# Feed-forward: where the two Silus of a part's first pair stand on ScalarE

## The chip, the cores and the metric

The kernel runs on one core of one Trainium2 chip. The metric is the device time of one execution in microseconds, the median of several runs. The names of the engines are those of the profile: PE is TensorE (PEld its weight loads), DVE is VectorE, ACT is ScalarE, POOL is GpSimd, SP is SyncE, which issues the loads.

## The reference

Two sequences (256 and 512 tokens, width 1024) go through two layers. Each layer has a mixer (an mLSTM in layer 0, a sliding-window attention in layer 1) and then a gated feed-forward with a depthwise convolution over three tokens:

```python
def conv_ffn(h, w_up, conv_w, conv_b, w_down):
    u = h @ w_up                                  # 1024 -> 2 * 2816
    u = lax.conv_general_dilated(u, conv_w[:, None, :], ...) + conv_b
    g = u[..., :D_FF]
    val = u[..., D_FF:]
    return (jax.nn.silu(g) * val) @ w_down
```

Around it stand a modulated RMS norm and a residual: `x = x + g2 * conv_ffn(h, ...)`. All is fp32. The kernel reaches that precision on PE by splitting each operand in two parts (`whi`/`wlo` for weights, `zh`/`zl` and others for activations) and taking three products of four.

## The kernel before, in words

The 768 tokens are one row of columns. The 2816 channels of the gate and the 2816 of the value are cut into 11 **parts** of 256 channels. A part `p` does, in `up(p)`, two **pairs**: pair 0 is the gate's 256 channels, pair 1 the value's. Then, one part later, `down(*prev)` multiplies the finished product of the part before with its 256 rows of `w_down` and adds it to the residual.

A pair (`pair`, line 1272) computes two output rows of 128 channels for all 768 columns by a Strassen-like scheme with seven products. A product is a call of `quarters`: 12 matmuls of 128x384 (lines 1252, 1253, 1254: high by high, low by high, high by low). The names T1, T2, T3, T4, B11, B21, B22 stand for the seven right-hand quarters; `yh/yl` hold B11 and B21, `zh/zl` hold T1 to T4, `bq` holds B22. The products gather in four fixed PSUM banks, `a`, `e`, `b`, `d` (in the order lists below `ps_4595`, `ps_4596`, `ps_4597`, `ps_4598`). Three copies on ACT fork a running sum into another bank or out of it. In the order of the code of a pair with its own B11 (all parts but the first two):

- `a` takes B11; the first fork `b <- a` (line 1296) starts `b`.
- `e` takes T1, and `p5 <- e` (line 1301) keeps it.
- `b` takes T2; then **`d <- b` (line 1307)**, which T3 must wait for, since `d` gathers T3 on top of it.
- `a` takes B21 and is evicted by ACT (line 1260, two pieces).
- `d` takes T3, and **`u3 <- d` (line 1315)**, the pair's third copy; meanwhile `b` takes B22.
- DVE writes the second halves of the two rows (lines 1317 and 1318); `d` takes T4 and ACT evicts it (line 1260).

A scheduler that plans with a timeline orders each engine's instructions from the code's order and the data dependences, so the code's order is a wish, not the final row. It interleaves pairs with the `down` tiles of the part before (line 230, PSUM tiles `pa`, four buffers, evicted into the residual by DVE at line 690). `tc.issue_after(ins)` makes what is written inside it stand behind `ins`. Weights come through five `raw` buffers of 128x1024; `split` makes `whi` by a cast on ACT (line 236) and `wlo` by a subtraction on DVE (line 237). POOL makes the sums of weight quarters (lines 1280 to 1292).

Behind each pair, `up` runs the convolution for its two rows: one activation on ACT (line 1476) and two scalar_tensor_tensor on DVE (lines 1478, 1479) for a row. For pair 0 the two rows of the gate, `yrow[:, 0]` and `yrow[:, 1]`, then get a Silu in place on ACT (line 1503). For pair 1 POOL multiplies each row of the value with the Silu of the gate (line 1505), and the product is split into `g` (lines 236 and 237), which `down` reads one part later.

Part 0 is written out by hand (`head`) and takes no `pair`. Part 1's pairs have `rest=True`: their B11 and B21 were done early.

Of the kernel before, what the change touches and what calls it, by code (L numbers as in the profile page):

```python
# [12 lines left out]
AF = mybir.ActivationFunctionType  # L13
# [65 lines left out]
def col(t):  # L79

    return t + (GAP if t >= 256 else 0)
# [64 lines left out]
class Net:  # L146
# [1125 lines left out]
    def pair(self, pool, u, bank, rows, rest=False):  # L1272


        nc = self.nc
        r1, r2 = rows
        rb, ra = (self.load(u, h) for h in (1, 0))
        q = [t[:, 512 * i : 512 * (i + 1)] for t in (ra, rb) for i in range(2)]
        tt = nc.gpsimd.tensor_tensor
        tt(q[2], q[2], q[3], ALU.add)  # L1280
        if not rest:
            wa = self.split(ra)
        tt(q[0], q[2], q[0], ALU.subtract)  # L1283
        tt(q[1], q[1], q[0], ALU.subtract)
        s1h, s1l = (pool.tile([P, 512], R, tag=t, name=self.nm(t), bufs=1) for t in ("s1h", "s1l"))
        part = lambda w, i: [t[:, 512 * i : 512 * (i + 1)] for t in w]
        fork = r1[:, col(H) :]
        if not rest:
            fork = a = bank(0)
            self.quarters(a, part(wa, 0), self.B11, True)  # L1290
        self.fp_copy_split(s1h, s1l, q[2])
        tt(q[2], q[3], q[0], ALU.subtract)
        wc = self.split(ra)
        wb = self.split(rb)
        e, b = bank(1), bank(2)
        nc.scalar.copy(b, fork)
        p5 = self.tmp([P, H])

        def fifth():
            self.quarters(e, (s1h, s1l), self.T1, True)  # L1300
            nc.scalar.copy(p5, e)

        if not rest:
            fifth()
        self.quarters(b, part(wc, 0), self.T2, False)
        d = bank(3)
        nc.scalar.copy(d, b)  # L1307
        if rest:
            fifth()
        else:  # L1310
            self.quarters(a, part(wa, 1), self.B21, False)
            self.evict(r1, a)
        self.quarters(d, part(wb, 0), self.T3, False)
        u3 = self.tmp([P, H])
        nc.scalar.copy(u3, d)
        self.quarters(b, part(wc, 1), self.B22, False)
        nc.vector.tensor_tensor(r1[:, col(H) :], b, p5, ALU.add)
        nc.vector.tensor_tensor(r2[:, col(H) :], e, u3, ALU.add)
        self.quarters(d, part(wb, 1), self.T4, False)
        self.evict(r2, d)  # L1320

    def prepare(self, u0, l):

        flat = [z.rearrange("p j k t -> p (j k t)") for z in (self.zh, self.zl)]
        place = lambda j: [z[:, j : j + 1024] for z in flat]

        ahead = [place(12 * H), place(4 * H)]
        wa = place(0)
        spare = None
        if l:  # L1330

            spare = self.slab([P, 3072], R)
            wa = [spare[:, 1024 * (z + 1) : 1024 * (z + 2)] for z in range(2)]
        self.fp_copy_split(*wa, self.load(u0 + 1, 0))
        for i in range(0 if l else 2):
            self.fp_copy_split(*ahead[i], self.load(u0 + 3 + i, 0))
        return wa, ahead, spare
# [123 lines left out]
    def ffn(self, l, xt, pool, last_tile, apply, keep=None):  # L1461
        nc = self.nc
        u0 = U_FFN + l * NPART * 3
        early = self.prepare(u0, l)
        next(last_tile)

        urows = [self.slab([P, 4, TG]) for _ in range(2)]
        for urow in urows:
            nc.gpsimd.memset(urow[:, :, 256 : 256 + GAP], 0.0)

        behind = []

        def conv(u, y, ch):
            cb = self.cst(CB + l * 44 + ch)
            w = lambda tap: self.cst(CW + (l * 44 + ch) * 3 + tap)
            nc.scalar.activation(y, u, AF.Identity, bias=cb, scale=w(1))  # L1476
            stt = nc.vector.scalar_tensor_tensor
            stt(y[:, 1:], u[:, :-1], w(0), y[:, 1:], ALU.mult, ALU.add)  # L1478
            stt(y[:, :-1], u[:, 1:], w(2), y[:, :-1], ALU.mult, ALU.add)  # L1479

        def up(p):
            urow = urows[0] if p == 0 else urows[1]
            fixed = lambda i: self.bank[i][:, :H]
            if p == 0:
                eng = mybir.EngineType
                self.ready(HALVES[0])
                with self.tc.manual_schedule(engines={eng.PE, eng.Activation, eng.DVE}):
                    behind[:] = self.head(u0, last_tile, pool, urows, mark, early)
            for i in range(2):
                if p:  # L1490
                    rows = [urow[:, 2 * i + j] for j in range(2)]
                    with ExitStack() as order:
                        for ins in behind[2 * i :] if p == 1 else ():
                            order.enter_context(self.tc.issue_after(ins))
                        self.pair(pool, u0 + 3 * p + i, fixed, rows, rest=p == 1)
                if i == 0:
                    yrow = self.slab([P, 4, TG])
                    g = self.slab([P, 2, 2, TG], R)
                for j in range(2):
                    y = yrow[:, 2 * i + j]  # L1500
                    conv(urow[:, 2 * i + j], y, i * FC + 2 * p + j)
                    if i == 0:
                        nc.scalar.activation(y, y, AF.Silu)
                    else:
                        nc.gpsimd.tensor_tensor(y, y, yrow[:, j], ALU.mult)  # L1505
                        self.fp_copy_split(g[:, 0, j], g[:, 1, j], y)
            return g

        def mark(t):

            hi, _ = self.quarter(self.B11)
            self.mm(t, hi[0][:, :P], hi[0], True, True)

        def down(p, g):
            ws = (w for _, w in self.halves(u0 + 3 * p + 2))
            chunk = lambda w, i: [t[:, 512 * i : 512 * (i + 1)] for t in w]

            def tile(w, c, rng):
                s0, s1, _ = rng
                o = self.pa()[:, : s1 - s0]  # L1520
                cs = slice(c % 4 * P, (c % 4 + 1) * P)
                for i in range(2):
                    wh, wl = chunk(w, i)
                    gh, gl = (g[:, z, i, col(s0) : col(s0) + s1 - s0] for z in range(2))
                    self.mm(o, wh[:, cs], gh, i == 0, False)
                    self.mm(o, wh[:, cs], gl, False, False)
                    self.mm(o, wl[:, cs], gh, False, i == 1)
                self.resid(xt, o, l, 40, c, rng)

            if p < NPART - 1:  # L1530
                for h, w in enumerate(ws):
                    for rng in SAMPLE, PROMPT:
                        for c in range(4 * h, 4 * h + 4):
                            tile(w, c, rng)
                return
            ws = list(ws)
            for rng in RANGES:
                norm = Norm(self, xt, rng, apply, last=keep is None and rng is RANGES[-1], adds=None if keep is not None else nc.vector)
                for c in range(KC):
                    tile(ws[c // 4], c, rng)  # L1540
                    norm.square(c)
                    if keep is not None or rng is not RANGES[-1] or c < 3:
                        self.tick(0.65)
                if keep is not None:
                    self.save_x(xt, keep, rng)
                self.start(rng, norm.stages())

        prev = None
        for p in range(NPART):
            g = up(p)  # L1550
            if prev is not None:
                down(*prev)
            prev = (p, g)
        down(*prev)
# [175 lines left out]
```

## Time and profile before

| | |
|---|---|
| Runs | 1902.64, 1899.25, 1902.51 us; median 1902.51 us |
| Profiled execution | span 1900.1 us; no time beside the span is listed for it, and the median of the runs lies 2.4 us above this span |
| PE busy | 1812.0 us (95%) |
| DVE, ACT, POOL busy | 1413.8, 920.9, 491.0 us |
| Granted PE clock, mean | 0.983 |
| Silus (line 1503) | 44, mean 847 ns, 37.3 us in all |

The page gives the busy time of each engine, then the span in 40 slices, the DMA queues, the chain of waits that ended last, and groups of instructions by line. A group's row names the line, the engine, what is written and read, the number of instructions, the busy time, the mean of one in ns, the idle time of that engine just before them, and what ended most of that idle time. In a timeline each row is: start, duration, engine, line, operation, names, count, and in brackets the idle time before it with its releaser. Ends of matmuls are modelled, so an idle time of PE is counted from a modelled end.

### The profile page before, as it was taken

How to read it: one execution, taken by the hardware profiler on the slowest of the kernel's cores; microseconds unless marked ns; L12 is line 12 of the kernel's file. 1: busy time of each engine (PE TensorE's matmuls, PEld its weight loads, DVE VectorE, ACT ScalarE, POOL GpSimd, SP SyncE). 2: the span in 40 equal slices, each digit the busy share in tenths (PEclk: the TensorE clock that was granted, in tenths of full speed). 3: DMA queues.
4: the chain of work that ended last, by engine and by line, in shares of the span. 5: the costliest groups of instructions: out<-in, count | busy, mean ns of one | idle time of the engine just before them, and what ended most of it. 6: DMA issues, size and time to landing. Idle time of an engine off the chain costs nothing.

```text
span 1900.1 us, 29288 instructions
## 1 busy us (share of the span) xinstructions
PE 1812.0 (95%) x11354; PEld 1672.5 (88%) x11354; DVE 1413.8 (74%) x2310; ACT 920.9 (48%) x1849; POOL 491.0 (26%) x395
## 2 busy tenths in 40 slices
PE   7889999999999999999999999989989999999997
PEld 5787887888998999999999988879979999999996
DVE  4664776687589877777777768875998777777777
ACT  4633434343456444444444466773564444444443
POOL 3001000022013433333332303330133333333322
PEclk9888999999999999999999999999999999999998
DMA  8243655456412222222222321212222222222211
GB/s 321 66 141 113 210 166 165 153 167 199 144 55 89 67 67 67 67 67 67 67 67 79 112 81 48 84 58 90 78 78 77 68 67 67 67 67 67 67 34 67
DMA packets 64246, 184.49 MB, mean 97 GB/s; under 512 B 6167, under 2 KB 23831, under 8 KB 64108
## 3 DMA queue, kind: packets, MB, share of 16 engines
q1 hardware_dynamic: 64108, 182.63, 29.6%
q8 instruction: 89, 1.46, 0.3%
q14 instruction: 49, 0.40, 0.1%
HBM read 176.17 MB, written 6.43 MB: 96 GB/s over the span
## 4 chain that ended last, share of the span: by engine, by line
PE 76%; DVE 11%; issue 5%; ACT 4%; DMA 2%; POOL 2%; SPq 0%; POOLq 0%; ACTq 0%; DVEq 0%
PE pa L230 23%; PE ps L230 23%; PE ps L1252 10%; PE ps L1253 9%; PE ps L1254 9%; DVE wlo L237 2%; DMA bt<-brow 1%; DVE slab L690 1%; ACT t L1078 1%; DVE t L1069 1%; POOL nt L112 1%; DVE slab L1479 1%; DVE zl L1210 1%; DVE slab L1478 0%; DVE slab L237 0%
## 5 line engine op out<-in xcount | busy, mean ns | idle before, releaser
L236 ACT CAST whi<-raw 128x1024 fp32r<-128x1024 f32 x237 | 248.7, 1049 | 401.1 <-PE pa L230 200.3
L237 DVE TENSOR_TENSOR wlo<-raw,whi 128x1024 fp32r<-128x1024 f32 x237 | 330.7, 1395 | 113.5 <-ACT whi L236 112.8
L230 PE MATMUL pa<-slab,whi 128*128 128x256 f32 (+1 forms) x1472 | 344.8, 331 | 4.4 <-DVE slab L690 4.2
L230 PEld LDWEIGHTS pa<-slab,whi 128*128 128x128 f32 x1472 | 250.9, 188 | 31.4 <-DVE slab L690 5.8
L690 DVE SCALAR_TENSOR_TENSOR slab<-pa,mod,slab 128x256 f32<-128x256 f32 (+1 forms) x368 | 207.8, 592 | 67.5 <-PE pa L230 66.9
L230 PE MATMUL ps<-zh,whi 128*128 128x256 f32 (+2 forms) x688 | 233.6, 340 | 4.4 <-ACT whi L236 2.6
L230 PE MATMUL pa<-slab,wlo 128*128 128x256 f32 (+1 forms) x736 | 234.0, 330 | 0.0
L230 PE MATMUL ps<-zh,wlo 128*128 128x256 f32 (+2 forms) x688 | 228.6, 335 | 4.3 <-DVE wlo L237 4.3
L230 PE MATMUL ps<-zl,whi 128*128 128x256 f32 (+2 forms) x688 | 229.0, 334 | 1.6 <-DVE zl L536 0.9
L1252 PE MATMUL ps<-zh,whi 128*128 128x384 f32 x504 | 171.2, 340 | 14.3 <-ACT ps L1307 13.1
L1253 PE MATMUL ps<-zl,whi 128*128 128x384 f32 x504 | 169.8, 337 | 1.7 <-DVE zl L1210 1.7
L1254 PE MATMUL ps<-zh,wlo 128*128 128x384 f32 x504 | 169.0, 335 | 0.0
L230 PEld LDWEIGHTS pa<-slab,wlo 128*128 128x128 f32 x736 | 138.3, 188 | 13.0 <-DVE wlo L237 0.9
L230 PEld LDWEIGHTS ps<-zh,whi 128*128 128x128 f32 x688 | 132.7, 193 | 18.0 <-ACT whi L236 3.2
L230 PEld LDWEIGHTS ps<-zh,wlo 128*128 128x128 f32 x688 | 132.4, 192 | 15.1 <-DVE wlo L237 5.1
L230 PEld LDWEIGHTS ps<-zl,whi 128*128 128x128 f32 x688 | 132.5, 193 | 11.2 <-DVE zl L536 1.3
L1505 POOL TENSOR_TENSOR slab<-slab 128x772 f32<-128x772 f32 x44 | 83.3, 1893 | 206.7 <-DVE slab L1479 193.9
L1283 POOL TENSOR_TENSOR raw<-raw,raw 128x512 f32<-128x512 f32 x40 | 52.1, 1303 | 294.1 <-DVE wlo L237 244.1
L1478 DVE SCALAR_TENSOR_TENSOR slab<-slab,cstt,slab 128x771 f32<-128x771 f32 x88 | 105.3, 1199 | 26.9 <-ACT slab L1476 26.9
L1479 DVE SCALAR_TENSOR_TENSOR slab<-slab,cstt,slab 128x771 f32<-128x771 f32 x88 | 119.7, 1360 | 0.8
L472 DVE SCALAR_TENSOR_TENSOR ada<-raw,silc,ada 128x1024 f32<-128x1024 f32 x84 | 114.0, 1387 | 6.5 <-DMA raw<-in_adaln_w_dram 6.3
L1252 PEld LDWEIGHTS ps<-zh,whi 128*128 128x128 f32 x504 | 94.7, 188 | 22.2 <-ACT ps L1307 18.2
(309 smaller groups left out, 4182.4 us busy)
## 6 DMA issues: line engine op xcount, KB each, us to landing
raw<-in_w_dram SPq DMA_DIRECT2D x208, 512.0 KB, 3.7
raw<-in_adaln_w_dram SPq DMA_DIRECT2D x84, 512.0 KB, 4.4
slab<-in_x_dram SPq DMA_DIRECT2D x12, 512.0 KB, 7.6
slab<-in_adaln_w_dram SPq DMA_DIRECT2D x12, 512.0 KB, 10.9
slab<-mrows SPq DMA_DIRECT2D x8, 384.0 KB, 5.7
xs<-slab SPq DMA_DIRECT2D x6, 512.0 KB, 2.9
bt<-brow SPq DMA_DIRECT2D x16, 192.0 KB, 3.2
slab<-xs SPq DMA_DIRECT2D x6, 512.0 KB, 6.7
```

What stands on the lines that cost most here:

```text
L230: self.last_mm = self.nc.tensor.matmul(out, lhsT, rhs, start=start, stop=stop)
L236: nc.scalar.copy(hi, src)
L237: return nc.vector.tensor_tensor(lo, src, hi.bitcast(F32), ALU.subtract)
L472: stt(acc[:, s], row, w, acc[:, s], ALU.mult, ALU.add)
L690: self.nc.vector.scalar_tensor_tensor(x, o, self.mod[l][:, gc + c, q : q + 1], x, ALU.mult, ALU.add)
L1252: mm(o, wh[:, k], hi[k], start=start and k == 0, stop=False, skip_group_check=True)
L1253: mm(o, wh[:, k], lo[k], start=False, stop=False, skip_group_check=True)
L1254: mm(o, wl[:, k], hi[k], start=False, stop=k == 3, skip_group_check=True)
L1283: tt(q[0], q[2], q[0], ALU.subtract)
L1478: stt(y[:, 1:], u[:, :-1], w(0), y[:, 1:], ALU.mult, ALU.add)
L1479: stt(y[:, :-1], u[:, 1:], w(2), y[:, :-1], ALU.mult, ALU.add)
L1505: nc.gpsimd.tensor_tensor(y, y, yrow[:, j], ALU.mult)
```

## The change

The two Silus of pair 0 are no longer written behind that pair's convolution, but behind the whole of pair 1's `pair` call, ahead of pair 1's convolution. In the parts from 1 on they stand inside `issue_after(third)`, where `third` is pair 1's third copy (`u3 <- d`), which `pair` now returns. In part 0, which has no `pair`, they are only written later.

```diff
         self.quarters(d, part(wb, 0), self.T3, False)
         u3 = self.tmp([P, H])
-        nc.scalar.copy(u3, d)
+        third = nc.scalar.copy(u3, d)
         self.quarters(b, part(wc, 1), self.B22, False)
...
         self.evict(r2, d)
+        return third.ins
...
-                        self.pair(pool, u0 + 3 * p + i, fixed, rows, rest=p == 1)
+                        third = self.pair(pool, u0 + 3 * p + i, fixed, rows, rest=p == 1)
                 if i == 0:
                     yrow = self.slab([P, 4, TG])
                     g = self.slab([P, 2, 2, TG], R)
+                if i:
+                    with self.tc.issue_after(third) if p else ExitStack():
+                        for j in range(2):
+                            nc.scalar.activation(yrow[:, j], yrow[:, j], AF.Silu)
                 for j in range(2):
                     y = yrow[:, 2 * i + j]
                     conv(urow[:, 2 * i + j], y, i * FC + 2 * p + j)
-                    if i == 0:
-                        nc.scalar.activation(y, y, AF.Silu)
-                    else:
+                    if i:
                         nc.gpsimd.tensor_tensor(y, y, yrow[:, j], ALU.mult)
                         self.fp_copy_split(g[:, 0, j], g[:, 1, j], y)
```

In the changed file the lines behind 1315 carry numbers higher by 1 to 3; the convolution is at 1477, 1479 and 1480, the Silu by chance at 1503 again.

The order of the instructions shows what the scheduler made of it. First ACT in part 7 of layer 0, pair 1 (`slab_8119` holds that part's `yrow`; `s1h_8412` is the cast of the next pair's weight sum; `whi_8263` and `whi_8333` are the two halves of `w_down` for the part before). Before:

```order
L1503 ACTIVATE slab_8119<-slab_8119 128x772
L236 CAST whi_8161<-raw_8129 128x1024
L1260 COPY slab_5199<-ps_4598 128x128
L1260 COPY slab_5199<-ps_4598 128x256
L1476 ACTIVATE slab_8119<-slab_5199,cstt 128x772
L236 CAST s1h_8412<-raw_8401 128x512
L1301 COPY nt_8166<-ps_4596 128x384
L1503 ACTIVATE slab_8119<-slab_8119 128x772
L1307 COPY ps_4598<-ps_4597 128x384
L236 CAST whi_8263<-raw_8261 128x1024
L1260 COPY slab_5199<-ps_4595 128x128
L1260 COPY slab_5199<-ps_4595 128x256
```

The third copy (line 1315) and the cast `whi_8333` are the next two rows there. In the changed kernel the same place reads:

```order
L236 CAST s1h_8412<-raw_8401 128x512
L1301 COPY nt_8164<-ps_4596 128x384
L1307 COPY ps_4598<-ps_4597 128x384
L236 CAST whi_8263<-raw_8261 128x1024
L1260 COPY slab_5199<-ps_4595 128x128
L1260 COPY slab_5199<-ps_4595 128x256
L1315 COPY nt_8217<-ps_4598 128x384
L1503 ACTIVATE slab_8119<-slab_8119 128x772 x2
L236 CAST whi_8333<-raw_8331 128x1024
L1477 ACTIVATE slab_8119<-slab_5199,cstt 128x772
```

The first Silu left its place between two weight casts, the second its place right ahead of `d <- b` (line 1307); both now stand between the third copy and the cast `whi_8333`. The same holds in parts 3 to 9 of both layers. From the middle of part 2's first pair on, the rows of PE, DVE, POOL and SP are, names aside, the same as before, up to the last `down` of the layer.

Second, DVE behind part 1's pairs, where `down` of part 0 runs between them and part 2's first pair (`wlo_6018` and `s1l_6131`, later `s1l_6129`, are weights of part 2; `pa` are the tiles of `down`). Before:

```order
L690 SCALAR_TENSOR_TENSOR slab_4605<-pa_5933,mod_88,slab_4605 128x512
L690 SCALAR_TENSOR_TENSOR slab_4605<-pa_5941,mod_88,slab_4605 128x512
L237 TENSOR_TENSOR wlo_6018<-raw_5991,whi_6017 128x1024
L690 SCALAR_TENSOR_TENSOR slab_4605<-pa_5949,mod_88,slab_4605 128x512
L690 SCALAR_TENSOR_TENSOR slab_4605<-pa_5957,mod_88,slab_4605 128x256
L237 TENSOR_TENSOR slab_5738<-slab_5737,slab_5738 128x772
L690 SCALAR_TENSOR_TENSOR slab_4605<-pa_5965,mod_88,slab_4605 128x256
L690 SCALAR_TENSOR_TENSOR slab_4605<-pa_5973,mod_88,slab_4605 128x256
L237 TENSOR_TENSOR s1l_6131<-raw_6119,s1h_6130 128x512
```

And in the changed kernel:

```order
L690 SCALAR_TENSOR_TENSOR slab_4605<-pa_5933,mod_88,slab_4605 128x512
L237 TENSOR_TENSOR wlo_6018<-raw_5991,whi_6017 128x1024
L237 TENSOR_TENSOR s1l_6129<-raw_6117,s1h_6128 128x512
L690 SCALAR_TENSOR_TENSOR slab_4605<-pa_5941,mod_88,slab_4605 128x512
L690 SCALAR_TENSOR_TENSOR slab_4605<-pa_5949,mod_88,slab_4605 128x512
L690 SCALAR_TENSOR_TENSOR slab_4605<-pa_5957,mod_88,slab_4605 128x256
L237 TENSOR_TENSOR slab_5738<-slab_5737,slab_5738 128x772
L690 SCALAR_TENSOR_TENSOR slab_4605<-pa_5965,mod_88,slab_4605 128x256
L690 SCALAR_TENSOR_TENSOR slab_4605<-pa_5973,mod_88,slab_4605 128x256
```

Two weight subtractions moved ahead of the eviction of `pa_5941`. The PE's row changes there too: T1 of part 2's first pair is done ahead of tile `pa_5941`, and part 1's T3 and B22 ahead of the second matmuls of a `down` tile. Layer 1 has the same. Beside these, PE, DVE and ACT rows are reordered from the last `down` of layer 0 into the attention's first projections, in the attention's softmax statistics (DVE) and slightly in the last norm.

## The prediction

> **What bounds the kernel now.** I read the page's busy shares first, then the waits of PE by stretch, then the timelines of ACT, PE and DVE at the places that the order list shows as changed.
>
> ```profile
> span 1900.1 us, 29288 instructions
> PE 1812.0 (95%) x11354; PEld 1672.5 (88%) x11354; DVE 1413.8 (74%) x2310; ACT 920.9 (48%) x1849; POOL 491.0 (26%) x395
> 640.00:1010.00 370.00, 364.74 (x2073) 345.59 (x2073) 283.50 (x317) 170.74 (x267) 132.67 (x78) 1.00 0.21 67
> 1480.00:1815.00 335.00, 329.75 (x1875) 312.50 (x1873) 258.08 (x287) 154.47 (x242) 120.38 (x72) 1.00 0.21 67
> ```
>
> The last two rows are windows over the steady feed-forward parts of layer 0 and layer 1: length, busy time of PE, PEld, DVE, ACT, POOL, then the granted clock. PE is missing 5.3 us in each, the clock is whole, and ACT works less than half of the time. So only what PE waits for counts there. The view of waits, PE alone, in the same two windows has one row each, and it accounts for all of the missing time:
>
> ```profile
> PE ps L1252 <- ACT ps L1307: 5.3, 7, 0.8
> PE ps L1252 <- ACT ps L1307: 5.3, 7, 1.0
> ```
>
> Seven times in each layer (parts 3 to 9, pair 1) T3's first matmul waits for the copy `d <- b` (line 1307), 10.6 us in all. Why the copy is late shows in ACT's timeline, part 7 of layer 0:
>
> ```profile
> 881.29 0.47 ACT L1301 COPY nt<-ps 128x384 f32<-128x384 f32 x1
> 883.56 0.85 ACT L1503 ACTIVATE slab<-slab 128x772 f32<-128x772 f32 x1 [1.80 <-DVE slab L1479]
> 884.32 0.47 ACT L1307 COPY ps<-ps 128x384 f32<-128x384 f32 x1
> 884.73 1.04 ACT L236 CAST whi<-raw 128x1024 fp32r<-128x1024 f32 x1
> 885.67 0.53 ACT L1260 COPY slab<-ps 128x128 f32<-128x128 f32 x2
> 887.24 0.48 ACT L1315 COPY nt<-ps 128x384 f32<-128x384 f32 x1 [1.03 <-PE ps L1254]
> 889.18 1.05 ACT L236 CAST whi<-raw 128x1024 fp32r<-128x1024 f32 x1 [1.46 <-PE ps L1253]
> 890.13 1.03 ACT L1476 ACTIVATE slab<-slab,cstt 128x772 f32<-128x772 f32 x1
> ```
>
> ACT stands idle from 881.8 until the second Silu's row is convolved at 883.5, runs the Silu, and only then the copy. But the copy could not have run in that idle time either, as PE's timeline of the same moment shows:
>
> ```profile
> 883.41 0.33 PE L1254 MATMUL ps<-zh,wlo 128*128 128x384 f32 x1
> 883.59 0.34 PE L1253 MATMUL ps<-yl,whi 128*128 128x384 f32 x1
> 883.76 0.34 PE L1254 MATMUL ps<-yh,wlo 128*128 128x384 f32 x1
> 884.85 0.45 PE L1252 MATMUL ps<-zh,whi 128*128 128x384 f32 x1 [0.75 <-ACT ps L1307]
> ```
>
> The row at 883.41 is T2's last matmul, the one that completes `b`. Only two matmuls of B21 stand between it and T3. So PE's own order keeps a part of the wait, whatever ACT does.
>
> **The change part by part.** *The copy in parts 3 to 9.* No instruction is added or removed: 44 Silus before and after, and no table load more or less. With the Silu gone from its front, the copy waits for T2 alone. How soon it then starts shows where it does so already, in part 2's first pair (PE's row, then ACT's):
>
> ```profile
> 631.54 0.33 PE L1254 MATMUL ps<-zh,wlo 128*128 128x384 f32 x1
> 631.92 0.46 ACT L1307 COPY ps<-ps 128x384 f32<-128x384 f32 x1 [1.17 <-PE ps L1254]
> ```
>
> 0.38 us from the start of T2's last matmul to the start of the copy. In part 7 that gives 883.41 + 0.38 = 883.79, the copy's 0.47 to 884.26, and PE 0.06 later (884.85 against the copy's end at 884.79) at 884.32. The two B21 matmuls end at 884.10, so 0.22 us of wait stays, of 0.75. Fourteen such waits: 10.6 - 14 x 0.22 = 7.5 us saved. The rows of PE, DVE, POOL and SP between these places are the same before and after, so what PE does behind T3 moves forward as a block. Next late would be the copy behind T2 itself.
>
> The Trainium skill's "TensorE: Matmul & The Clock Gate", section "Single matmul latency", puts a warm matmul with 384 columns at (398 + 384) / 2.4 = 326 ns from start to result; as an estimate by that page the copy could start about 0.05 us earlier than the 0.38 of the trace, and the 14 waits would shrink by another 0.7 us. The measured pair of rows is used.
>
> *The Silus at their new place, parts 2 to 10.* They stand behind the third copy, S = 887.24, in the 1.46 us in which ACT waits for PE to let go of a `whi` buffer. By the steps above (copy to next instruction 0.41, Silu to next 0.76) they run at S + 0.41 and S + 1.17, and the cast can start at S + 1.93; today it starts at S + 1.94. So they just fill the hole: 0. Upper bound if they didn't, one step of 0.76 per part; see the third rival. Who else waits for them: POOL's product, which starts at 893.63 for another reason, the value's convolution on DVE, 4 us after the Silus would end:
>
> ```profile
> 893.63 1.86 POOL L1505 TENSOR_TENSOR slab<-slab 128x772 f32<-128x772 f32 x1 [6.78 <-DVE slab L1479]
> ```
>
> Behind the cast stand a convolution activation and the next cast; SP's and POOL's queues are not moved past by anything. The first Silu's old slot lay ahead of a cast that waits for POOL anyway, so its leaving changes nothing: 0.
>
> ```profile
> 877.31 0.84 ACT L1503 ACTIVATE slab<-slab 128x772 f32<-128x772 f32 x1
> 878.32 1.06 ACT L236 CAST whi<-raw 128x1024 fp32r<-128x1024 f32 x1 [0.17 <-POOL raw L1292]
> ```
>
> *Part 1, where the order of DVE and PE changes, both layers.* Today:
>
> ```profile
> 624.93 1.40 DVE L690 SCALAR_TENSOR_TENSOR slab<-pa,mod,slab 128x512 f32<-128x512 f32 x2
> 626.25 1.83 DVE L237 TENSOR_TENSOR wlo<-raw,whi 128x1024 fp32r<-128x1024 f32 x1
> 628.00 1.13 DVE L690 SCALAR_TENSOR_TENSOR slab<-pa,mod,slab 128x512 f32<-128x512 f32 x2
> 630.71 0.68 DVE L237 TENSOR_TENSOR s1l<-raw,s1h 128x512 fp32r<-128x512 f32 x1
> 631.71 1.21 DVE L237 TENSOR_TENSOR wlo<-raw,whi 128x1024 fp32r<-128x1024 f32 x1
> 626.54 0.41 PE L230 MATMUL pa<-slab,whi 128*128 128x256 f32 x2
> 628.80 0.51 PE L230 MATMUL pa<-slab,whi 128*128 128x256 f32 x2 [0.85 <-DVE slab L690]
> 629.61 0.34 PE L1252 MATMUL ps<-zh,whi 128*128 128x384 f32 x1
> 625.15 1.85 POOL L1505 TENSOR_TENSOR slab<-slab 128x772 f32<-128x772 f32 x1 [0.97 <-DVE slab L1479]
> ```
>
> There are four `pa` buffers, so tile `pa_5973` (626.54) needs the eviction of `pa_5941`, and the last, `pa_5981` (628.80), that of `pa_5949`. DVE is behind here and PE pays 0.85 us. In the new row the eviction of `pa_5941` stands behind the `wlo` and the `s1l`: 624.93 + 0.70 = 625.63 for `pa_5933`, + 1.83 + 0.68 + 0.70 = 628.84. Tile `pa_5973` starts then instead of at 626.54; its 0.71 us and the last tile's 0.81 (628.80 to 629.61) bring T2 to 630.3 instead of 629.61, **+0.7 us**. Bounds: with the `wlo` at its undisturbed 1.21 us +0.1; if DVE caught up before this point the wait that is there now goes, -0.85. If the `wlo`, which would start in the middle of POOL's product (625.15 to 627.00), had to wait for its end, 627.00 + 1.21 instead of 627.46, +1.5. I take 0.7, the duration that this `wlo` has at this place today; twice, +1.4 us.
>
> The Trainium skill's "SBUF — State Buffer", section "SBUF: two separate sides", speaks against the change here: DVE operations with two SBUF inputs and POOL's reads share a port pair under an exclusive lock, and the loser blocks. By that rule the upper bound holds, 3.0 us for both layers instead of 1.4, and the whole comes to 1898.0. The row at 626.25 bears it out in kind: 1.83 against 1.21 us while POOL runs.
>
> *Part 1's own T3* moves ahead of two `down` matmuls, with no wait before or behind it: 0. *The layer boundary*, from the last `down` of layer 0 into the attention. The view of waits, PE, 1030 to 1120 us:
>
> ```profile
> PE pa L230 <- POOL nt L112: 1.3, 2, 1.0
> PE pa L230 <- DVE slab L690: 1.2, 3, 0.4
> PE ps L230 <- DVE zl L516: 0.7, 2, 0.6
> ```
>
> 3.2 us of waits in the reordered stretch. The same tiles in another order may lose or gain; no row says which. Bounds -3.2 to +3.2, value 0.
>
> **The sum:** -7.5 + 0 + 1.4 + 0 = -6.1 us against the profiled span of 1900.1, so 1894.0. The median of the runs, 1902.5, lies 2.4 above that span, so **1896.4 us**.
>
> **The rivals.** *The gain is given back in the reordered places.* Part 1 at its upper bound in both layers (+3.0) and the boundary at +3.2 leave 7.5 - 6.2 = 1.3 us: 1901.2. For it: DVE is behind in part 1 today, and POOL's product runs in just that moment. Against it: it needs both at their ends.
>
> *T3 no longer waits at all.* If the copy were out of T3's way wholly, 10.6 would go, and with +1.4 the time is 1893.3. Against it: PE's row still has only two matmuls between T2 and T3, and the copy's 0.47 us don't fit.
>
> *The Silus delay the cast of the second half of `w_down`, and through it DVE.* The hole is 1.46 us and two Silu steps are 1.52, so it has no slack. Behind the cast:
>
> ```profile
> 889.36 0.56 DVE L1317 TENSOR_TENSOR slab<-ps,nt 128x384 f32<-128x384 f32 x1 [0.97 <-PE ps L1254]
> 890.27 1.23 DVE L237 TENSOR_TENSOR wlo<-raw,whi 128x1024 fp32r<-128x1024 f32 x1 [0.35 <-ACT whi L236]
> 892.46 1.02 DVE L1479 SCALAR_TENSOR_TENSOR slab<-slab,cstt,slab 128x771 f32<-128x771 f32 x1
> 894.26 0.75 DVE L690 SCALAR_TENSOR_TENSOR slab<-pa,mod,slab 128x512 f32<-128x512 f32 x1 [0.78 <-PE pa L230]
> ```
>
> DVE takes its `wlo` 0.04 us after the cast, and has 0.78 us to spare before it must evict `pa` tiles. If the cast were late by a whole Silu pair, 1.52, 0.74 us a part would reach PE's `pa` tiles; in the 18 parts 2 to 10 that is 13.3 us, and 1902.5 - 6.1 + 13.3 = 1909.7. It eats the whole gain from 6.1 / 18 = 0.34 us a part on, a cast late by 0.78 + 0.34 = 1.1 us. For it: every part would pay. Against it: by the steps the cast is on time to 0.01.
>
> **How the numbers follow.** Forecast 0.74, given back 0.14, no wait left 0.04, cast late 0.08. The low end is the forecast with part 1's wait gone in both layers (-0.85 for +0.7, twice: -3.1) and 1.8 of the boundary's 3.2 us: 1891.5. The high end is the given-back case, 1901.2. About 0.2%, 3.8 us, is what can be told from no change; that is 1898.7. The forecast lies above it with 0.04 of its chance, the given-back case wholly: faster 0.74, same 0.18, slower 0.08.
>
> **What would show it.** Right: PE's waits for line 1307 in the two windows fall from 5.3 to about 1.5 each with nothing new beside them; the copy follows T2's last matmul by 0.38 us; the cast behind the Silus starts at S + 1.9. In part 1 of each layer PE waits for line 690 about 1.5 to 2 us at `pa_5973`. Wrong: a new row in the two windows (line 690 or a `wlo`), a cast later than S + 2.5, or waits at the layer boundary far from 3.2 us.

## The result, and the profile after

The changed kernel takes 1896.11 us (median of 10 runs, 1889.54 to 1899.11), the kernel before 1902.58 us (10 runs, 1899.25 to 1906.30). The ratio is 0.9965, 95% interval 0.9956 to 0.9975: 6.5 us faster, between 4.8 and 8.4. The profiled execution has a span of 1895.3 us and took 1897.17 us.

The head of the page, and the windows over the two steady stretches (length, then busy time of PE, PEld, DVE, ACT, POOL):

```profile
span 1895.3 us, 29265 instructions
PE 1810.2 (96%) x11354; PEld 1670.8 (88%) x11354; DVE 1403.6 (74%) x2310; ACT 920.4 (49%) x1849; POOL 503.7 (27%) x395
640.00:1010.00 370.00, 368.60 (x2096) 349.61 (x2095) 283.46 (x319) 172.31 (x271) 132.87 (x79) 1.00 0.22 69
1480.00:1815.00 335.00, 333.60 (x1894) 315.78 (x1893) 256.40 (x288) 153.71 (x241) 122.71 (x71) 1.00 0.21 68
```

PE now misses 1.4 us in each window where it missed 5.3. The waits of PE in the same windows, one row each:

```profile
PE ps L1252 <- ACT ps L1307: 1.4, 7, 0.2
PE ps L1252 <- ACT ps L1307: 1.4, 7, 0.2
```

The same seven places a layer, each at 0.2 us, and nothing new beside them. Part 7 of layer 0, pair 1, in PE's timeline and then in ACT's:

```profile
881.34 0.33 PE L1254 MATMUL ps<-zh,wlo 128*128 128x384 f32 x1
881.51 0.34 PE L1253 MATMUL ps<-yl,whi 128*128 128x384 f32 x1
881.69 0.34 PE L1254 MATMUL ps<-yh,wlo 128*128 128x384 f32 x1
882.23 0.45 PE L1252 MATMUL ps<-zh,whi 128*128 128x384 f32 x1 [0.20 <-ACT ps L1307]
882.51 0.34 PE L1253 MATMUL ps<-zl,whi 128*128 128x384 f32 x1
```

```profile
881.71 0.46 ACT L1307 COPY ps<-ps 128x384 f32<-128x384 f32 x1 [1.97 <-PE ps L1254]
882.09 1.05 ACT L236 CAST whi<-raw 128x1024 fp32r<-128x1024 f32 x1
883.04 0.54 ACT L1260 COPY slab<-ps 128x128 f32<-128x128 f32 x2
884.62 0.48 ACT L1315 COPY nt<-ps 128x384 f32<-128x384 f32 x1 [1.04 <-PE ps L1254]
885.00 1.59 ACT L1503 ACTIVATE slab<-slab 128x772 f32<-128x772 f32 x2
886.56 1.05 ACT L236 CAST whi<-raw 128x1024 fp32r<-128x1024 f32 x1
```

The copy starts 0.37 us after T2's last matmul, ends at 882.17, and T3 starts 0.06 later. The two Silus stand as one row of two behind the third copy (884.62), and the cast behind them starts 1.94 us after that copy.

**Where each microsecond went.** Matmul number n of PE's row can be found in every trace by counting, so the time from one matmul's start to another's compares stretches with the same number of matmuls. "Start" is the first matmul. The bounds are named by the times of before's trace. "Last norm" is the stretch 1850 to 1890. The kernels e1 to e8 are those of the next section.

| us from start to start | start to 560 | 610 to 648 (part 1, layer 0) | 648 to 1005 (steady) | 1005 to 1120 (boundary) | 1425 to 1447 (part 1, layer 1) | 1490 to 1800 (steady) | last norm |
|---|---|---|---|---|---|---|---|
| before | 550.19 | 38.06 | 356.88 | 115.07 | 22.03 | 310.02 | 41.66 |
| after | 549.95 | 38.54 | 353.00 | 116.95 | 22.51 | 306.19 | 43.63 |
| e1 Silus moved from part 3 on | 547.48 | 38.41 | 353.00 | 118.44 | 22.03 | 306.19 | 43.76 |
| e2 second Silu alone | 546.76 | 38.07 | 353.00 | 116.94 | 22.02 | 306.19 | 43.64 |
| e3 first Silu alone | 545.50 | 38.53 | 357.80 | 116.94 | 22.51 | 309.92 | 41.95 |
| e4 after, B21 behind T2 | 547.96 | 38.53 | 349.86 | 115.38 | 22.53 | 303.05 | 41.95 |
| e5 after, once more | 548.97 | 38.53 | 353.00 | 115.40 | 22.51 | 306.19 | 43.63 |
| e6 e1, B21 behind T2 | 545.97 | 38.13 | 349.88 | 115.37 | 22.03 | 303.05 | 42.00 |
| e7 Silus moved in layer 0 | 547.47 | 38.53 | 353.00 | 116.92 | 22.03 | 310.75 | 42.00 |
| e8 before, B21 behind T2 | 544.73 | 38.07 | 349.66 | 119.17 | 22.04 | 303.13 | 41.96 |

Two columns vary between executions of one kernel: after and e5 are the same program and differ by 1.0 us up to 560 and by 1.55 at the boundary. The other columns repeat to 0.01 us in those two. So, after against before: steady -3.88 and -3.83, part 1 +0.48 in each layer, last norm +1.97. Together -4.8. Of the stretches that the table leaves out, 1120 to 1425 and 1447 to 1490 differ between after and e5 as well, by 1.7 and 0.5 us. What the boundary and the first of these owe to the granted clock is worked out below.

### The profile page after: what moved, and what is told of

The parts are those of the page before. It is cut to its first block, busy times and chain, and to the rows that moved or that the text cites. A ratio compares the mean times of both kernels' runs of the same rounds, so it can differ in the third digit from the quotient of the medians.

```text
span 1895.3 us, 29265 instructions
## 1 busy us (share of the span) xinstructions
PE 1810.2 (96%) x11354; PEld 1670.8 (88%) x11354; DVE 1403.6 (74%) x2310; ACT 920.4 (49%) x1849; POOL 503.7 (27%) x395
## 5 line engine op out<-in xcount | busy, mean ns | idle before, releaser
L237 DVE TENSOR_TENSOR wlo<-raw,whi 128x1024 fp32r<-128x1024 f32 x237 | 319.6, 1349 | 110.2 <-ACT whi L236 109.3
L230 PEld LDWEIGHTS ps<-zh,whi 128*128 128x128 f32 x688 | 131.7, 192 | 18.9 <-ACT whi L236 4.2
L230 PEld LDWEIGHTS ps<-zh,wlo 128*128 128x128 f32 x688 | 131.6, 191 | 14.6 <-DVE wlo L237 4.7
L1508 POOL TENSOR_TENSOR slab<-slab 128x772 f32<-128x772 f32 x44 | 87.4, 1987 | 190.8 <-DVE slab L1480 179.4
L1280 POOL TENSOR_TENSOR raw<-raw 128x512 f32<-128x512 f32 x40 | 64.9, 1622 | 184.9 <-DMA raw<-in_w_dram 177.2
```

What stands on the lines that cost most here:

```text
L230: self.last_mm = self.nc.tensor.matmul(out, lhsT, rhs, start=start, stop=stop)
L237: return nc.vector.tensor_tensor(lo, src, hi.bitcast(F32), ALU.subtract)
```

## The experiments

Eight kernels. Beside e1 to e4, on one chip, before took 1902.82 us (18 runs); beside e5 to e8, on another, 1901.65 (17 runs). Line numbers behind 1307 shift by one to a few in kernels with added lines.

**e1_late3**: the Silus move only in parts 3 to 10.

```diff
+        stay = lambda p, j: p < 3
...
                         for j in range(2):
+                            if not stay(p, j):
                                 nc.scalar.activation(yrow[:, j], yrow[:, j], AF.Silu)
...
                     conv(urow[:, 2 * i + j], y, i * FC + 2 * p + j)
+                    if i == 0 and stay(p, j):
+                        nc.scalar.activation(y, y, AF.Silu)
                     if i:
```

> The Silus move only in parts 3 and up; part 1 and part 2 keep the row of before on PE and DVE. If the gain is the shorter wait for the copy of line 1307 (my theory), the 14 waits fall to 0.2 us each as in the changed kernel, and the 0.8 to 1.2 us that part 1 lost in each layer is not paid: -7.5 us in the feed-forward parts, and -5.5 to -7.5 us in all, since the last norm keeps the reordered row that cost about 2 us in the changed kernel's profile. Rival, the gain comes from the reordered rows at part 1 and the layer boundary: about 0 in the 14 waits and less than half of the gain.

Measured: 1896.56 us (5 runs), ratio 0.9969, interval 0.9958 to 0.9981. The steady stretches are those of the changed kernel to 0.01 us. Part 1 keeps its order and PE's wait there its 0.9 us. In the time, nothing of that is seen: 1896.56 against 1896.11. About 1 us for part 1 is below what these intervals can show; the matched stretches show it in layer 1 (22.03 against 22.51). In layer 0 a different short wait takes most of it back (38.41).

**e2_second_only** and **e3_first_only**: one of the two Silus stays where it was. With the lines of e1, `stay` is `j == 0` in e2 and `j == 1` in e3.

> Only the second Silu of each part goes behind the third copy, the first stays where it was. Theory: the second Silu alone stands between T2 and the copy, so the 14 waits fall to 0.2 us as with both, -7.5 us there, and -5.5 to -7.5 us in all. Rival, what matters is ACT's load ahead of the copy or that the hole behind the third copy is filled: then one Silu of two brings about half, -3 us.

> Only the first Silu goes behind the third copy, the second stays right ahead of the copy of line 1307. Theory: the 14 waits stay at 5.3 us for each layer, and what is left is the reordered part 1: 0 to +2 us against the kernel before. Rival (each Silu carries half): -3 us.

Measured: e2 1895.66 us (6 runs), ratio 0.9970, 0.9957 to 0.9982; e3 1903.38 us (12 runs), ratio 1.0006, 0.9995 to 1.0017. The waits of PE in e3, layer 0's and layer 1's steady stretch:

```profile
PE ps L1252 <- ACT ps L1307: 6.2, 7, 1.2
PE ps L1252 <- ACT ps L1307: 5.2, 7, 0.8
```

In e2 both rows read 1.4, 7, 0.2 as in the changed kernel. So the whole gain hangs on the second Silu, the one that stood right ahead of `d <- b`. The first one's move gains nothing; in part 1 it is the first one's move that brings the new order (38.53 and 22.51, as in the changed kernel).

**e4_b21_behind_t2**: the changed kernel, with B21's 12 matmuls held behind T2 on PE, so that they lie between T2 and T3.

```diff
-            mm(o, wl[:, k], hi[k], start=False, stop=k == 3, skip_group_check=True)
+            self.last = mm(o, wl[:, k], hi[k], start=False, stop=k == 3, skip_group_check=True)
...
         self.quarters(b, part(wc, 0), self.T2, False)
+        t2 = self.last.ins
...
-            self.quarters(a, part(wa, 1), self.B21, False)
+            with self.tc.issue_after(t2):
+                self.quarters(a, part(wa, 1), self.B21, False)
```

> The changed kernel, with B21's 12 matmuls (all parts with an own B11) held behind T2's last, so that 12 instead of 2 of them lie between T2 and T3. Theory: what is left of each wait is PE's own order; 12 matmuls take 2.1 us and hide the copy's 0.38 + 0.47 + 0.06 us, so the 14 waits vanish. Each costs 0.54 us from start to start where 0.18 is the pace, and the next matmul another 0.1, so -6 us beside the changed kernel, about -12 to -14 us beside the kernel before. Rival, another wait takes its place (the eviction of a, DVE's rows): no better than the changed kernel, -6.5 us.

Measured: 1888.19 us (6 runs), ratio 0.9928, 0.9917 to 0.9940, 14.6 us below before. PE waits for nothing in either steady stretch, and they are 3.14 us shorter each than in the changed kernel. Yet the waits that went were only 1.4 each. The timeline of the changed kernel above holds the difference: a wait of 0.20 us makes the step from 881.69 to 882.23, 0.54 where an undisturbed one is 0.17 to 0.18 (881.51 to 881.69), and the next step (882.23 to 882.51) is 0.28. Together 0.47 us lost for 0.20 shown, seven times 3.3. The whole gain is a little more than the 12 to 14 expected, and not all of it is B21's: of the 7.9 us between e4 and the changed kernel 6.3 stand in the steady stretches and 1.7 in the last norm (41.95 against 43.63), where the scheduler's row came out another way.

**e5_after_again**: the changed kernel on the chip of the following three.

> The changed kernel as it is, beside the three that follow on the same chip. Expected: 1896.5 us, 6 to 6.5 below before; PE's waits for line 1307 1.4 to 1.5 us in each of the two steady windows; 2.5 us of waits for DVE at line 112 in the last norm.

Measured: 1895.48 us (8 runs), ratio 0.9963, 0.9947 to 0.9978, 6.2 us below before.

**e6_late3_b21**: e1 and e4 together.

> The Silus moved from part 3 on only, and B21's 12 matmuls held behind T2 in every pair with its own B11. Part 1 keeps the order of before, and so does the last norm. Theory (the copy's way from T2 to T3 is what is left of the wait, and part 1's new order costs 0.8 to 1.2 us a layer): no PE wait in either steady window, and 1 to 2 us faster than the same kernel with the Silus moved in all parts, which was 14.6 us below before; so 15.5 to 16.5 below before, 1886 to 1887.5. Rival (part 1's new order is free, since the Silus in parts 1 and 2 only changed which of two waits stands there): equal to the other within 0.7 us, 1888 to 1889.

Measured: 1886.64 us (4 runs), ratio 0.9917, 0.9903 to 0.9932, 15.0 us below before, and no wait in the steady stretches. e4 stood 14.6 below its own before, so the times do not tell theory and rival apart. The matched stretches do for part 1: 38.13 and 22.03 against e4's 38.53 and 22.53, so its order costs 0.4 to 0.5 us a layer, half of what the theory took and not nothing. It has the lowest median here; e4's and e8's intervals overlap with it.

**e7_layer0_only**: `stay` is `l == 1`.

> The Silus moved in layer 0 only. Theory (14 equal and independent waits, 0.55 us of each saved): layer 0's steady window shows 1.5 us of waits for line 1307, layer 1's keeps 5.3; the last norm keeps a short wait (1.2 us at line 112); time -3.85 for the waits and +0.8 for part 1 of layer 0, 3 us below before, 1899.5 to 1900. Rival (the time saved in layer 0 is lost again at the reordered layer boundary): within 1 us of before.

Measured: 1898.70 us (10 runs), ratio 0.9983, 0.9972 to 0.9995, 3.0 us below before. PE's waits in the steady stretch of layer 0, then of layer 1:

```profile
PE ps L1252 <- ACT ps L1307: 1.4, 7, 0.2
PE ps L1252 <- ACT ps L1307: 5.9, 7, 0.9
```

Each layer saves its own part: layer 0's matched stretches give -3.88 + 0.48 = -3.4, and 3.0 is measured, so the gain is not lost again at the boundary. Layer 1's steady stretch, with the Silus where they were, took 310.75 against before's 310.02, with 5.9 us of waits against 5.3; no run says why.

**e8_b21_alone**: the lines of e4 in the kernel before, the Silus written where they were.

> The Silus written where they were before, and only B21's 12 matmuls held behind T2; the scheduler then puts the second Silu behind the copy d <- b, ahead of the next weight cast. Theory (what ends the wait is work of PE between T2 and T3; 12 matmuls are 2.1 us, more than the 0.38 + 0.47 + 0.06 us of the copy's way, wherever the Silus are): no wait for line 1307 in the steady windows, 10 to 12 us below before, 1891 to 1893. Rival (the Silus must stand behind the third copy, else they push a cast or the copy itself): waits for line 1307, or new ones for line 690 or a wlo, of 3 us and more in each window, 1896 or above.

Measured: 1888.64 us (6 runs), ratio 0.9927, 0.9914 to 0.9941, 13.0 us below before: more than the theory's 10 to 12. The windows over the steady stretches, the second and third numbers being length and PE's busy time:

```profile
640.00:1005.00 365.00, 365.00 (x2085) 348.01 (x2084) 282.92 (x319) 170.25 (x267) 135.23 (x79) 1.00 0.22 69
1470.00:1800.00 330.00, 330.00 (x1892) 315.12 (x1891) 259.10 (x288) 153.21 (x242) 125.79 (x73) 1.00 0.21 68
```

PE is whole there, without the change that this case is about. ACT at the corresponding place of part 7:

```profile
872.55 0.46 ACT L1308 COPY ps<-ps 128x384 f32<-128x384 f32 x1 [0.40 <-PE ps L1254]
873.96 0.85 ACT L1505 ACTIVATE slab<-slab 128x772 f32<-128x772 f32 x1 [0.94 <-DVE slab L1481]
874.71 1.03 ACT L236 CAST whi<-raw 128x1024 fp32r<-128x1024 f32 x1
```

Given another row for PE, the scheduler put the second Silu behind the copy by itself. So this is not a pure test of B21 with the Silu still in front. It shows that writing the Silus in another place is not needed once the copy has 12 matmuls beside it. No run keeps the second Silu ahead of the copy with those 12 matmuls in place. The miss in size is again the loss that the view of waits does not show: the steady stretches fell by 7.22 and 6.89, 14.1, for 10.6 us of shown waits, 0.25 more for each of the 14.

## Why the prediction was right, step by step

**The copy in parts 3 to 9: right.** -7.5 was forecast, the matched stretches give -7.7. The step "0.38 from T2's last matmul to the copy" measured 0.37, the copy 0.46 for 0.47, T3 0.06 behind it, the rest of the wait 0.20 for 0.22. That a wait costs more than its row did no harm here, since each wait only became shorter and its fixed loss stayed. By the 0.05 us earlier start that the Trainium skill's "TensorE: Matmul & The Clock Gate", section "Single matmul latency", led to as an estimate, the 14 waits would have ended at about 2.4 us; 2.8 is measured. The row had the right size; the page's figure runs only to the result, not to the copy's start, and the page states it for a bf16 matmul, where the operands here are fp32r.

**The Silus at their new place: right.** The cast starts at S + 1.94 (S + 1.93 forecast). The `wlo` behind it and the eviction that follows are where they were, with the same 0.35 and 0.78 us to spare:

```profile
887.65 1.23 DVE L237 TENSOR_TENSOR wlo<-raw,whi 128x1024 fp32r<-128x1024 f32 x1 [0.35 <-ACT whi L236]
891.64 0.75 DVE L690 SCALAR_TENSOR_TENSOR slab<-pa,mod,slab 128x512 f32<-128x512 f32 x1 [0.78 <-PE pa L230]
```

**Part 1: the size came out, the working did not.** +0.7 a layer was forecast. In the ten microseconds around the `pa` tiles it is +0.71 (10.03 to 10.74 in layer 0, 9.92 to 10.63 in layer 1); the stretch ahead of them is 0.12 and 0.23 shorter, and in layer 0 0.11 comes back behind them, so +0.48 net. PE's wait is the one that was named, in its timeline and in DVE's and POOL's at the same time:

```profile
628.32 0.51 PE L230 MATMUL pa<-slab,whi 128*128 128x256 f32 x2 [1.68 <-DVE slab L690]
623.04 0.74 DVE L690 SCALAR_TENSOR_TENSOR slab<-pa,mod,slab 128x512 f32<-128x512 f32 x1
623.70 1.66 DVE L237 TENSOR_TENSOR wlo<-raw,whi 128x1024 fp32r<-128x1024 f32 x1
625.28 2.32 DVE L237 TENSOR_TENSOR s1l<-raw,s1h 128x512 fp32r<-128x512 f32 x1
627.53 1.79 DVE L690 SCALAR_TENSOR_TENSOR slab<-pa,mod,slab 128x512 f32<-128x512 f32 x3
624.24 2.81 POOL L1508 TENSOR_TENSOR slab<-slab 128x772 f32<-128x772 f32 x1
```

The forecast gave the `s1l` its undisturbed 0.68 us; it took 2.32, and ended 0.55 behind POOL's product (627.05). That alone would have made the wait 1.6 us longer. But DVE came to this place 1.4 us earlier. PE is 0.47 earlier here than in before's trace, so before's eviction of `pa_5933` at 624.93 would stand at 624.46, and it stands at 623.04. Those two cancel, within 0.2. The gain in time has its source some 8 us earlier. DVE and POOL there, before:

```profile
614.73 1.01 DVE L1479 SCALAR_TENSOR_TENSOR slab<-slab,cstt,slab 128x771 f32<-128x771 f32 x1
615.66 0.48 DVE L690 SCALAR_TENSOR_TENSOR slab<-pa,mod,slab 128x256 f32<-128x256 f32 x1
616.05 2.76 DVE L237 TENSOR_TENSOR wlo<-raw,whi 128x1024 fp32r<-128x1024 f32 x1
615.88 1.85 POOL L1505 TENSOR_TENSOR slab<-slab 128x772 f32<-128x772 f32 x1 [9.78 <-DVE slab L1479]
```

And in the changed kernel:

```profile
614.49 1.01 DVE L1480 SCALAR_TENSOR_TENSOR slab<-slab,cstt,slab 128x771 f32<-128x771 f32 x1
615.41 1.22 DVE L237 TENSOR_TENSOR wlo<-raw,whi 128x1024 fp32r<-128x1024 f32 x1
616.55 0.87 DVE L690 SCALAR_TENSOR_TENSOR slab<-pa,mod,slab 128x256 f32<-128x256 f32 x2
615.64 2.71 POOL L1508 TENSOR_TENSOR slab<-slab 128x772 f32<-128x772 f32 x1 [9.78 <-DVE slab L1480]
```

Whichever of the two starts first runs at its own length, and the other is longer by about the overlap. POOL's product is released by the second convolution on DVE (its bracket). Before, DVE's row has the eviction of one `pa` tile between that convolution and the `wlo`; in the changed kernel that eviction stands behind the `wlo`, which so starts before the product does. The prediction passed over this swap: that is the step that was missing, together with the `s1l`'s true length. The rule of the Trainium skill's "SBUF — State Buffer", section "SBUF: two separate sides", that the loser blocks for the whole instruction agrees with these rows (the `wlo` of before ends 1.08 after POOL's, and one undisturbed takes 1.22). The `s1l` above agrees too: it ends 0.55 behind the product, and an undisturbed one takes 0.68. The upper bound of +1.5 a layer, drawn from the rule for the `wlo` alone, was not reached, because at 623.70 the `wlo` started ahead of the product (624.24) and the `s1l` was the loser.

**The layer boundary: +0.3 for the forecast 0, and a scatter that is the clock's.** PE's waits there sum to 3.7 us against 3.2. The stretch takes 116.95 us against 115.07, but 115.40 for the same program once more. The same matmuls in before, in the changed kernel and in e5, then 3.4 us of the changed kernel's stretch, with the granted clock as the third number from the end:

```profile
1005.03:1120.10 115.07, 111.85 (x806) 106.99 (x805) 83.21 (x144) 58.02 (x111) 22.85 (x23) 1.00 0.30 94
1001.28:1118.23 116.95, 113.25 (x806) 108.51 (x806) 83.07 (x144) 57.96 (x111) 24.73 (x23) 0.99 0.29 92
999.34:1114.74 115.40, 111.66 (x806) 106.94 (x805) 83.09 (x144) 57.88 (x111) 24.77 (x23) 1.00 0.30 94
1056.98:1060.38 3.40, 3.40 (x19) 3.40 (x18) 1.45 (x3) 1.29 (x4) 2.19 (x3) 0.50 0.14 48
```

In the changed kernel's trace the granted clock is 0.50 from 1056.98 to 1060.38, and half of such a dip of 3.4 us is 1.7. The traces without such a dip in this stretch need 115.07 (before) and 115.37 to 115.40 (e4, e5, e6), those with one 116.92 to 116.95 (after, e2, e3, e7), those with two 118.44 (e1) and 119.17 (e8). So the reordering itself costs about 0.3 us. The attention's reordered statistics, for which the prediction had no term, cost nothing that can be seen: from 1120 to 1425 before needs 304.96 us and e5 304.89, each with one dip, after 303.23 without one.

**The last norm: missed.** The prediction gave it no term, though the text on the change names its reordering. It costs 1.97 us. The waits of PE from 1850 us to the end, before, and the matmul of the norm at which the two kernels part:

```profile
PE pa L230 <- POOL nr L131: 2.7, 2, 2.5
PE pa L230 <- DVE slab L690: 1.3, 3, 0.5
PE pa L230 <- DVE nt L112: 0.9, 2, 0.6
1887.42 0.38 PE L230 MATMUL pa<-inv,nt 128*128 128x2 f32 x2 [0.26 <-DVE nt L112]
```

The waits of the changed kernel at the same matmuls, from 1843.4 us to the end:

```profile
PE pa L230 <- DVE nt L112: 2.5, 2, 1.9
PE pa L230 <- POOL nr L131: 2.0, 2, 1.8
PE pa L230 <- DVE slab L690: 1.3, 3, 0.5
```

The sums are 4.9 and 5.8, so this view shows half of the loss. DVE and PE in the changed kernel show the place:

```profile
1880.66 1.26 DVE L690 SCALAR_TENSOR_TENSOR slab<-pa,mod,slab 128x256 f32<-128x256 f32 x3
1881.84 0.42 DVE L112 TENSOR_TENSOR nt<-nt,nt 128x256 f32<-128x256 f32 x1
1882.31 0.61 PE L230 MATMUL pa<-inv,nt 128*128 128x2 f32 x4 [1.91 <-DVE nt L112]
```

Three evictions in a row stand ahead of the last sum (line 112) that the norm's matmul needs; before, evictions and sums alternate. The wait at this matmul grew from 0.26 to 1.91 us, 1.65 of the 1.97. From it to the last group of matmuls it is 4.78 us against 4.46, with a granted clock of 0.57 against 0.85; the wait for POOL that stands there is shorter (1.79 against 2.52), which is why the sums differ by less. The kernels with DVE's row in this order (after, e1, e2, e5) need 43.6 to 43.8 us for the stretch, the five other experiments 41.95 to 42.0, before 41.66. That ties the loss to the order; no kernel changed that order alone. In the same four PE's row differs from before's as well, but only behind the matmul at which the 1.65 are lost.

**The sum.** -6.1 forecast, -6.5 and -6.2 measured. The terms as measured give -7.7 + 1.0 + 0.3 + 2.0 = -4.4, just outside the first interval (-8.4 to -4.8) and inside e5's (-10.1 to -4.2). So the agreement owes something to luck: a missed +2.0 and the boundary's +0.3 stand against part 1's net +1.0 for +1.4 and a remainder of some 2 us that the runs do not place. The stretches that vary between executions by 1 us and more can hide it.

## What to carry to other kernels

When a wait names one late instruction, look at the whole way from the last producer to the waiting consumer, on both engines: here 0.37 + 0.46 + 0.06 us stood against two matmuls of cover, and giving PE 12 matmuls in that place took 14.1 us from the steady stretches where hurrying the copy took 7.7. A kernel ordered by a scheduler reorders far from the edit; each reordered stretch needs a term of its own, and counting matmuls between fixed places in two traces prices each to a tenth of a microsecond where the span of one execution varies by several, if the granted clock of the stretch is read beside it. Two engines that shut each other out make a term that hangs on who starts first, so give it both signs.

## What the runs showed of the hardware that was not expected

- A stall of PE costs more than its row in the view of waits. Busy ends of matmuls overlap (0.34 us long, started every 0.17 to 0.18), so an idle time counted from the modelled end leaves 0.16 out, and the first step after the wait was 0.28 us, 0.10 more. Removing 14 waits of 10.6 us shown shortened the steady stretches by 14.1 us in e8.
- DVE's subtraction of 128x1024 took 1.22 us when it started 0.23 ahead of POOL's product and 2.76 when it started 0.17 behind it; the product took 2.71 and 1.85 us.
- At the layer boundary the granted clock fell to 0.50 for about 3.4 us at a time, never, once or twice in an execution of whichever kernel, and the stretch took 115.1 to 115.4, 116.9 or 118.4 and more.
- The part before 560 us, with PE's row the same in all ten profiled executions, took 544.7 to 550.2 us; its granted clock, 0.96 to 0.97, does not order the times. Its spread of 5.5 us is nearly the whole gain of this change, which is why one span says little here.
